# A hybrid pooling and linear-attention block on one core: both head pairs of the state part in step, GpSimd left with weight sums alone, tiles on multiples of 128 bytes

## The chip, the cores and the metric

The kernel runs on one core of a Trainium2 chip. The metric is the time of one execution in microseconds on the device; the median of three runs is given. The core has a matrix engine (TensorE, PE in the profile, with its weight loads as PEld), VectorE (DVE), ScalarE (ACT), GpSimd (POOL), and a queue (SP) that issues all transfers. Each engine works through its own instructions in order and waits on semaphores for the others.

## The reference

```
u = rmsnorm(h, norm_mix);  z = u @ w_in
a, q, k, v, r, lr, ga, gb = split(z)          # 512, 256, 256, 512, 512, 16, 1024, 1024 columns
p   = per group: (trailing mean over 2, 4, 8 or 16 tokens of a) - a;  p = (p @ w_pool_mix) * pool_scale
y_a = p @ w_pool_out
log_a = log_sigmoid(lr @ w_gate_up + b_gate) / 16
# per head (4 heads, 64 key and 128 value columns), over chunks of 64 tokens:
o     = scores_with_decay @ v + (q * exp(b)) @ S;   S = exp(b_end) * S + (k * exp(b_end - b))^T @ v
o   = rmsnorm(o, gla_norm) * silu(r);  y_b = o @ w_gla_out
h   = h + (sigmoid(ga) * y_a + sigmoid(gb) * y_b) @ w_out
h   = h + relu(rmsnorm(h, norm_ffn) @ w_ff1)^2 @ w_ff2
out = rmsnorm(h, norm_final)                  # 1024 tokens, 1024 wide, 16 leading meta tokens dropped
```

## The kernel before

Every large product is made from operands split in two: a high part (`th`, `w1h`, ...), which ACT rounds with a copy, and a low part (`tl`, `w1l`, ...), the difference, which DVE or POOL takes. Three matmuls (L258 to L260: high by high, high by low, low by high) make one product; most are 512 columns wide. A *filler matmul* below is one of these three.

The program runs through these stages. The *opening* (`start`) normalizes eight tiles of 128 tokens, transposes them on PE (L244, identity `ident`), splits them (`th` L200, `tl` L201), and makes the values v, tile by tile (`v_tile`), with the weight halves `vw[0]` and `vw[1]`, which `load_vw` loads through the two `raw` buffers and splits. `lrraw` is sixteen more columns of weights. `warm` makes matmuls of a blank tile. Then come the pooling columns and keys (a ring `W1` of two weight slots is filled by `Ring.top_up`: load, ACT copy L75, subtraction L76 on the engine `W1.eng`). The *pairs of projections* take weights two blocks of 128 columns at a time by a seven-product scheme: `sums_weights` forms sums and differences of weight quarters (`fs`, `s3`, L640 to L646, on POOL), `split` (L598, L599) makes their two parts, three products ahead of use. Between products `inside` runs the decay part of the attention (`gi`, `N`, `F`, L812, L840 to L880), a generator whose pieces are let out by time credits (`STRETCH`). At its end `pooled_part` brings the pooled rows back (`pm_dram`) and splits them into the old `th` and `tl` (L751, L752).

The *state part* (`gla`) runs four units `across(p, half)`: head pair p of 0 and 1, half of the tokens 0 and 1. A unit transposes the keys (L1036), makes the chunk products kv (L1042), runs eight state steps on DVE (L1048), multiplies scores by v (L1055) and queries by states (L1065), squares on ACT (`on`, L1071), reduces (L1073), takes an inverse root (small operations, L209 to L218), scales (L1075), transposes back (L1079), and multiplies by the gate (`sr`, L1080; `yg`, L1082, L1083). At each `yield` it names a time, and `pour` lets out filler matmuls for `PACE` times that long: first the blocks of y_a (`ya_block`: gate exp L950, product with the gate L976, a store to `ma_dram`), then those of y_b for the first half (`yb_block`: L1005, L1006, then `th` and `tl`, L1009 and L1010). Units start one after another, two alive at most:

```
UNITS = [(0, 0), (1, 0), (0, 1), (1, 1)]
...
if waiting and len(live) < 2 and since > 1:
    live.append(waiting.pop(0))
```

The merge, the first feed-forward layer and the second follow; nothing in them is rewritten.

The order on PE is the order of the code. The order on the other engines and on the SP queue is set by a scheduler that works from priorities and readiness, so an edit can move instructions that it does not name. Tiles come from a left-hand stack (from low addresses up) and a right-hand one (from the top down); a tile that is popped gives its place to later ones.

Of the kernel before, what the change touches and what calls it, by code (L numbers as in the profile page):

```python
# [31 lines left out]
PACE, LEVEL, OPENING, STRETCH = 1.6, 1.6, 6.0, 1.9  # L32
# [71 lines left out]
def kernel(  # L104
# [58 lines left out]
    small = left.push("small", [P, 144], F32)  # L163
    small_at = [0]

    def tiny(n):
        a = small_at[0]
        small_at[0] += n
        assert small_at[0] <= 144
        return small[:, a : a + n]  # L170
# [155 lines left out]

    def load_vw(i):
        vw, n = S["vw"][i], 256 + 16 * (i == 0)
        for j in range(2):
            r = raw.load(w_cols(C_V + i * 256 + j * P), D).rearrange("p (k c) -> p k c", k=KT)  # L330
            c = slice(j * P, (j + 1) * P)
            act.activation(vw[:, 0, :, c], r, ACT.Copy)
            eng = pool if i else dve
            eng.tensor_tensor(vw[:, 1, :, c], r, f32(vw[:, 0, :, c]), ALU.subtract)
        if i == 0:
            r = S["lrraw"]
            act.activation(vw[:, 0, :, 256:], r, ACT.Copy)
            pool.tensor_tensor(vw[:, 1, :, 256:], r, f32(vw[:, 0, :, 256:]), ALU.subtract)
# [44 lines left out]
    def start():  # L383
# [3 lines left out]
        S["lrtok"] = left.push("lrtok", [P, 9, 16], F32)  # L387
# [19 lines left out]
        W1.eng = pool  # L407
        for t in range(8):
            if 0 < t < 6:
                load(t + 2)  # L410
            if t == 1:
                nc.sync.dma_start(xm, meta)
            if t == 3:
                W1.top_up()
            u = us[:, t % 3]
            layer_norm(xs[:, t % 4], u)
            transposed(u, t // 4, OFF[t // 4] + (t % 4) * P, ("ms", "sc"))
            if t == 0:
                nc.sync.dma_start(S["lrraw"], w_in[:, C_LR : C_LR + 16].rearrange("(k p) c -> p k c", p=P))
                load_vw(0)  # L420
                load(1)
                load(2)
                load_vw(1)
                warm(10, P)
            if t == 6:
                layer_norm(xm, um)
            if t < 3:
                v_tile(0, t)
            else:
                for i, n in SPREAD[t]:  # L430
                    v_tile(i, n)
# [9 lines left out]
        W1.eng = dve  # L441
# [12 lines left out]
    def pool_open():  # L454
# [11 lines left out]
        pool.tensor_tensor(mw[:, 1], r, f32(mw[:, 0]), ALU.subtract)  # L466
# [51 lines left out]
    def differences():  # L518
# [9 lines left out]
        def parts(p, a, eng=dve):  # L528
            hi, lo = x[p]
            act.activation(hi, a, ACT.Copy)  # L530
            eng.tensor_tensor(lo, a, f32(hi), ALU.subtract)

        dve.tensor_tensor(b11, b12, b11, ALU.subtract)
        pool.tensor_tensor(b12, b22, b12, ALU.subtract)
# [3 lines left out]
        parts("P7", b12, pool)  # L538
# [91 lines left out]
    def sums_weights(order, n_pairs, load, eng):  # L630

        for p, i in order(n_pairs):
# [3 lines left out]
            else:  # L636
                a21, a22 = (w1raw[i, 1][:, k : k + 4] for k in (0, 4))
                s = quad(S["fs"][:, i % 2] if p != "P7" else S["s3"])
                if p == "P5":
                    eng.tensor_tensor(s, a21, a22, ALU.add)  # L640
                elif p == "P6":
                    eng.tensor_tensor(s, s, a11, ALU.subtract)
                elif p == "P7":
                    eng.tensor_tensor(s, a11, a21, ALU.subtract)
                elif p == "P3":
                    eng.tensor_tensor(s, a12, s, ALU.subtract)  # L646
                elif p == "P4":
                    s = a22
# [24 lines left out]
    def pairs_of_projections():  # L673
# [18 lines left out]
        for n, (p, i, (ah, al)) in enumerate(ahead(pair_weights(), 3)):  # L692
# [30 lines left out]
            if n > 8:  # L723
                credit += 12 * 512 / 2400 / STRETCH
                while credit > 0 and chain:
                    w = next(chain, None)
                    if w is None:
                        chain = None
                    else:
                        credit -= w  # L730
# [4 lines left out]
            if total - n == 3:  # L735
                raw.back()
                W1.shift, W1.eng = 1, pool
# [3 lines left out]

    def pooled_part(g):

        S["pm"] = [t[0].rearrange("p k c -> p (k c)")[:, : 4 * SEQ].rearrange("p (g c) -> p g c", g=4) for t in (TH, TL)]
        spare = [t.rearrange("p n b -> p (n b)") for t in (*S["N"], S["F"])]
        for n in range(3) if g == 0 else (3,) if g == 1 else ():
            nc.sync.dma_start(
                spare[n % 3].rearrange("p (h c) -> p h c", h=2), pm_dram[n].rearrange("h p c -> p h c")
            )
        ph, pl = (t[:, g] for t in S["pm"])  # L750
        act.activation(ph, spare[g % 3], ACT.Copy)  # L751
        pool.tensor_tensor(pl, spare[g % 3], f32(ph), ALU.subtract)  # L752
# [141 lines left out]
    UNITS = [(0, 0), (1, 0), (0, 1), (1, 1)]  # L894

    def gla_open():
        W1.eng = pool
# [86 lines left out]
    def yb_block(j, h):  # L984
        def fn(wb):
# [4 lines left out]
            for e in range(2):  # L990
# [19 lines left out]
                pool.tensor_tensor(tl, gl, f32(th), ALU.subtract)  # L1010
# [9 lines left out]
    seen = [tiny(2) for _ in range(2)]  # L1020

    def across(p, half):
# [11 lines left out]
        b = quad(bank("ms"))  # L1034
# [3 lines left out]
        yield 1.6  # L1038
# [10 lines left out]
        yield 4.4  # L1049
# [10 lines left out]
        dve.tensor_copy(seen[p], o[:, :, 3, P - 1])  # L1060
# [15 lines left out]
        yield 6.0  # L1076
# [11 lines left out]
    def gla():  # L1088
# [14 lines left out]
        waiting, live, since = [across(*u) for u in UNITS], [], 9  # L1103
        while waiting or live:
            if waiting and len(live) < 2 and since > 1:
                live.append(waiting.pop(0))
                since = 0
            since += 1
            waits = [(g, next(g, None)) for g in live]
            live = [g for g, w in waits if w is not None]  # L1110
            pour(max([w for _, w in waits if w is not None], default=0) * PACE)
# [6 lines left out]
    def merge_open():  # L1118
        W1.eng = dve
# [298 lines left out]
    tails = [(tiny(1), tiny(1)) for _ in range(4)]  # L1418
# [101 lines left out]
```

## Time and profile before

| | |
|---|---|
| median of 3 runs | 1281.24 us (1277.63 to 1282.63) |
| the profiled execution | 1280.45 us, its span 1278.7 us |
| mean granted TensorE clock | 0.986 |
| busy: PE, DVE, ACT, POOL | 1231.0, 853.4, 634.3, 141.1 us |
| moved | 192 MB, 150 GB/s over the span |

The stages in the profile, by the first instructions of each: opening 0 to 40 us, pooling and keys to 158, pairs of projections to 401 with their last products to 417.5, state part to about 534, merge to 640, then the feed-forward layers. Line numbers are those of the kernel before. A row of the profile names the engine, the line, the tile written and the tiles read. A releaser behind an arrow is what ended the idle time ahead of an instruction.

### The profile page before, as it was taken

To read this page: it belongs to the slowest core of one execution; us is meant where nothing else is said; L and a number is where in the kernel's file an instruction comes from. 1 tells how busy PE (TensorE), PEld (TensorE's weight loads), DVE (VectorE), ACT (ScalarE), POOL (GpSimd) and SP (SyncE) were. 2 spreads that over 40 slices of the span, in tenths; PEclk is the share of its full clock that TensorE was granted. 3 is DMA by queue.
4 is the path that set the end of the run, shared out by engine and by line. 5 is a ranking of instruction groups with operands and counts; after the bars stand their busy time and mean duration, and the time that the engine had idled before them with its cause. 6 is when DMAs were issued, how large, how long until landed. Compare 5 with 4: busy or idle time off the path is not lost.

```text
span 1278.7 us, 18357 instructions
## 1 busy us (share of the span) xinstructions
PE 1231.0 (96%) x6795; PEld 1002.7 (78%) x6795; DVE 853.4 (67%) x1383; ACT 634.3 (50%) x1119; POOL 141.1 (11%) x89
## 2 busy tenths in 40 slices
PE   7999999999998989799999999999999999999997
PEld 6999876777777777588778888888878788888776
DVE  5525459786786356742797767767764777887686
ACT  6623456766666424531665544544554444444544
POOL 2110141222224115410000000000000000000000
PEclk8999999999999999899999999999999999999999
DMA  7312343433336974760234444444469863333532
GB/s 220 111 38 83 93 131 83 122 117 109 101 116 234 320 253 140 246 231 34 83 110 162 149 150 155 149 151 154 156 214 370 268 228 106 98 92 91 166 92 88
DMA packets 153402, 192.23 MB, mean 150 GB/s; under 512 B 12097, under 2 KB 89169, under 8 KB 153313
## 3 DMA queue, kind: packets, MB, share of 16 engines
q1 hardware_dynamic: 153312, 191.06, 46.7%
q8 instruction: 53, 0.87, 0.3%
q14 instruction: 37, 0.30, 0.1%
HBM read 129.14 MB, written 61.88 MB: 149 GB/s over the span
## 4 chain that ended last, share of the span: by engine, by line
PE 79%; DVE 7%; DMA 6%; ACT 4%; issue 3%; POOL 1%; SPq 0%; ACTq 0%; DVEq 0%; POOLq 0%
PE b_o L260 8%; PE b_o L259 8%; PE b_o L258 8%; PE b_mm L259 6%; PE b_mm L260 6%; PE b_mm L258 6%; PE b_y L258 5%; PE b_y L260 5%; PE b_y L259 5%; PE b_z L258 3%; PE b_z L259 3%; PE b_sc L258 3%; PE b_z L260 3%; PE b_sc L259 3%; PE b_sc L260 3%
## 5 line engine op out<-in xcount | busy, mean ns | idle before, releaser
L598 ACT ACTIVATE w1h<-raw 128x512 fp32r<-128x512 f32 x106 | 65.9, 624 | 62.7 <-PE b_y L259 19.5
L599 DVE TENSOR_TENSOR w1l<-raw,w1h 128x512 fp32r<-128x512 f32 x106 | 74.0, 698 | 23.3 <-ACT w1h L598 23.2
L258 PE MATMUL b_sc<-th,w1h 128*128 128x512 f32 x216 | 86.3, 400 | 2.4 <-ACT u2p L705 1.7
L258 PE MATMUL b_z<-th,w1h 128*128 128x512 f32 x216 | 85.9, 398 | 0.0
L259 PE MATMUL b_z<-tl,w1h 128*128 128x512 f32 x216 | 84.9, 393 | 0.4 <-DVE tl L1206 0.4
L259 PE MATMUL b_sc<-tl,w1h 128*128 128x512 f32 x216 | 84.7, 392 | 0.0
L260 PE MATMUL b_z<-th,w1l 128*128 128x512 f32 x216 | 84.6, 392 | 0.0
L260 PE MATMUL b_sc<-th,w1l 128*128 128x512 f32 x216 | 84.6, 391 | 0.0
L258 PE MATMUL b_o<-w1h 128*128 128x512 f32 x192 | 75.8, 395 | 2.9 <-DVE h L1346 1.9
L598 ACT ACTIVATE w1h<-fs 128x512 fp32r<-128x512 f32 x81 | 50.9, 628 | 54.5 <-PE b_y L259 30.8
L259 PE MATMUL b_o<-w1l,w1h 128*128 128x512 f32 x192 | 75.8, 395 | 1.3 <-DVE w1l L599 1.3
L599 DVE TENSOR_TENSOR w1l<-fs,w1h 128x512 fp32r<-128x512 f32 x81 | 60.6, 749 | 23.9 <-ACT w1h L598 23.8
L260 PE MATMUL b_o<-w1h,w1l 128*128 128x512 f32 x192 | 75.9, 395 | 0.1
L258 PE MATMUL b_mm<-th,w1h 128*128 128x512 f32 (+1 forms) x208 | 71.9, 346 | 3.5 <-DVE c L976 2.6
L259 PE MATMUL b_mm<-tl,w1h 128*128 128x512 f32 (+1 forms) x208 | 71.0, 342 | 0.0
L260 PE MATMUL b_mm<-th,w1l 128*128 128x512 f32 (+1 forms) x208 | 71.0, 341 | 0.0
L598 ACT ACTIVATE w1h<-bt 128x512 fp32r<-128x512 f32 x45 | 28.4, 630 | 57.5 <-issue 33.8
L1394 DVE TENSOR_TENSOR bt<-w,w 128x512 f32<-128x512 f32 x80 | 54.8, 685 | 2.4 <-DMA w<-in_w_ff_dram 2.4
L258 PEld LDWEIGHTS b_sc<-th,w1h 128*128 128x128 f32 x216 | 40.6, 188 | 13.4 <-ACT u2p L705 2.1
L258 PE MATMUL b_mm<-wo,th 128*128 128x512 f32 x128 | 50.7, 396 | 0.0
L259 PE MATMUL b_o<-fxl,fxh 128*128 128x512 f32 x128 | 49.8, 389 | 0.6 <-DVE small L217 0.6
L258 PE MATMUL b_o<-fxh 128*128 128x512 f32 x128 | 50.3, 393 | 0.0
(374 smaller groups left out, 3414.2 us busy)
## 6 DMA issues: line engine op xcount, KB each, us to landing
hf_dram<-h SPq DMA_DIRECT2D x112, 256.0 KB, 2.1
raw<-hf_dram SPq DMA_DIRECT2D x112, 256.0 KB, 2.7
w<-in_w_ff_dram SPq DMA_DIRECT2D x64, 256.0 KB, 4.9
raw<-in_w_in_dram SPq DMA_DIRECT2D x22, 512.0 KB, 4.8
raw<-in_w_ff_dram SPq DMA_DIRECT2D x16, 512.0 KB, 4.1
rawx<-in_w_ff_dram SPq DMA_DIRECT2D x16, 512.0 KB, 4.2
rawp<-in_w_in_dram SPq DMA_DIRECT2D x10, 512.0 KB, 4.7
xs<-in_x_dram SPq DMA_DIRECT2D x8, 512.0 KB, 5.5
```

Source lines behind the costliest of these rows:

```text
L258: pe.matmul(ps, ah, bh, start=first and i == 0, stop=False, skip_group_check=more)
L259: pe.matmul(ps, ah, bl, start=False, stop=False, skip_group_check=more)
L260: pe.matmul(ps, al, bh, start=False, stop=last and i == n - 1, skip_group_check=more)
L598: act.activation(hi, a, ACT.Copy)
L599: dve.tensor_tensor(lo, a, f32(hi), ALU.subtract)
L1394: dve.tensor_tensor(bt, w, S["w2"][q[3:]][:, i], ALU.add if q[2] == "+" else ALU.subtract)
```

## The change

It does five things. The units of the state part go in pairs: for each half both `across(0, half)` and `across(1, half)` advance together, and the times named and `PACE` are altered. POOL keeps the sums of weights, each as two instructions of half the width; its subtractions (L76 in the opening and the state part, the second half of `vw` and `lrraw`, L466, L531, L534, L752, L1010) go to DVE. In the opening the weights of `vw[1]` are asked for early and split later, and six more warm matmuls stand after tile 1. `pooled_rows` asks for pooled rows apart from splitting them. `small` shrinks from 144 to 128 columns and `lrtok` grows from 9 to 10 rows, so that left-hand tiles behind them begin on multiples of 128 bytes; two small scratch columns are reused to fit.

```diff
-PACE, LEVEL, OPENING, STRETCH = 1.6, 1.6, 6.0, 1.9
+PACE, LEVEL, OPENING, STRETCH = 1.3, 1.6, 6.0, 1.9
-    small = left.push("small", [P, 144], F32)
+    small = left.push("small", [P, 128], F32)
-        S["lrtok"] = left.push("lrtok", [P, 9, 16], F32)
+        S["lrtok"] = left.push("lrtok", [P, 10, 16], F32)
...
     def load_vw(i):
-            r = raw.load(w_cols(C_V + i * 256 + j * P), D).rearrange("p (k c) -> p k c", k=KT)
+            r = vw_raw[i][j]
-            eng = pool if i else dve
-            eng.tensor_tensor(vw[:, 1, :, c], r, f32(vw[:, 0, :, c]), ALU.subtract)
+            dve.tensor_tensor(vw[:, 1, :, c], r, f32(vw[:, 0, :, c]), ALU.subtract)
...
-        W1.eng = pool
         for t in range(8):
             if t == 0:
-                load_vw(0)
+                ask_vw(0)
                 load(1)
                 load(2)
-                load_vw(1)
                 warm(10, P)
+                load_vw(0)
+                ask_vw(1)
+            if t == 1:
+                warm(6, P)
+            if t == 2:
+                load_vw(1)
...
+        def tt(out, a, b, op):
+            for k in (slice(0, 2), slice(2, 4)) if eng is pool else (slice(0, 4),):
+                eng.tensor_tensor(out[:, k], a[:, k], b[:, k], op)
-                    eng.tensor_tensor(s, a21, a22, ALU.add)
+                    tt(s, a21, a22, ALU.add)
...
     def pooled_part(g):
-        pool.tensor_tensor(pl, spare[g % 3], f32(ph), ALU.subtract)
+        dve.tensor_tensor(pl, spare[g % 3], f32(ph), ALU.subtract)
...
     def gla_open():
-        W1.eng = pool
     def yb_block(j, h):
-                pool.tensor_tensor(tl, gl, f32(th), ALU.subtract)
+                dve.tensor_tensor(tl, gl, f32(th), ALU.subtract)
     def across(p, half):
-        b = quad(bank("ms"))
+        b = quad(bank("ms") if p == 0 else wide2()[:, 0])
-        yield 1.6
+        yield 1.4
-        yield 4.4
+        yield 5.0
-        yield 6.0
+        yield 8.0
     def gla():
-        waiting, live, since = [across(*u) for u in UNITS], [], 9
-        while waiting or live:
-            if waiting and len(live) < 2 and since > 1:
-                live.append(waiting.pop(0))
-                since = 0
-            since += 1
-            waits = [(g, next(g, None)) for g in live]
-            live = [g for g, w in waits if w is not None]
-            pour(max([w for _, w in waits if w is not None], default=0) * PACE)
+        for half in range(2):
+            live = [across(p, half) for p in range(2)]
+            while live:
+                waits = [(g, next(g, None)) for g in live]
+                live = [g for g, w in waits if w is not None]
+                pour(max([w for _, w in waits if w is not None], default=2.0) * PACE)
```

How it moves instructions, at three places. The first is DVE in the opening, from the end of the normalization of tile 1 (`us`) to tile 1's low parts (`tl`); `lrtok` belongs to the first tile of values. Before:

```order
L232 SCALAR_TENSOR_TENSOR us<-xs,small,gB 128x1024
L356 COPY lrtok<-b_mm 128x16
L213 SCALAR_TENSOR_TENSOR small<-small 128x1
L217 TENSOR_SCALAR small<-small 128x1
L218 TENSOR_TENSOR small<-small 128x1
L232 SCALAR_TENSOR_TENSOR us<-xs,small,gB 128x1024
L201 TENSOR_TENSOR tl_135<-b_sc,th_131 128x4x128
L210 TENSOR_SCALAR small<-small 128x1
L201 TENSOR_TENSOR tl_135<-b_ms,th_131 128x4x128
```

The same place on DVE now (`vw_190` is `vw[1]`):

```order
L232 SCALAR_TENSOR_TENSOR us<-xs,small,gB 128x1024
L362 COPY lrtok<-b_mm 128x16
L213 SCALAR_TENSOR_TENSOR small<-small 128x1
L340 TENSOR_TENSOR vw_190<-raw_115,vw_190 128x8x128
L217 TENSOR_SCALAR small<-small 128x1
L210 TENSOR_SCALAR small<-small 128x1
L218 TENSOR_TENSOR small<-small 128x1
L201 TENSOR_TENSOR tl_135<-b_sc,th_131 128x4x128
L201 TENSOR_TENSOR tl_135<-b_ms,th_131 128x4x128
L232 SCALAR_TENSOR_TENSOR us<-xs,small,gB 128x1024
L340 TENSOR_TENSOR vw_190<-raw_119,vw_190 128x8x128
```

One half of `vw[1]` came in ahead of tile 1's low parts, and the normalization of tile 2 went behind them.

The second place is PE at the start of the state part's second unit: `kt_3915` (now `kt_3971`) is the transposed key tile of head pair 1. Before, its kv products followed the first unit's query products:

```order
L1065 MATMUL b_m_4093<-w_3919,gi_3883 64x128 x4
L1065 MATMUL b_m_4093<-S,gi_3883 64x128
L1065 MATMUL b_m_4093<-w_3919,gi_3883 64x128
L1065 MATMUL b_m_4093<-S,gi_3883 64x128
L1065 MATMUL b_m_4093<-w_3919,gi_3883 64x128 x9
L1042 MATMUL b_sc<-v,kt_3915 64x128 x16
```

Now, on PE, they follow the first unit's kv, three products after the keys' transposes:

```order
L1053 MATMUL b_sc<-ident,gi_3943 128x128 x4
L258 MATMUL b_mm<-th_131,w1h 128x512
L259 MATMUL b_mm<-tl_135,w1h 128x512
L260 MATMUL b_mm<-th_131,w1l 128x512
L258 MATMUL b_mm<-th_131,w1h 128x512
L259 MATMUL b_mm<-tl_135,w1h 128x512
L260 MATMUL b_mm<-th_131,w1l 128x512
L258 MATMUL b_mm<-th_131,w1h 128x512
L259 MATMUL b_mm<-tl_135,w1h 128x512
L260 MATMUL b_mm<-th_131,w1l 128x512
L1059 MATMUL b_m_4076<-v,kt_3967 64x128 x16
L1059 MATMUL b_sc<-v,kt_3971 64x128 x16
```

The second unit's kv moved ahead by 33 + 12 filler matmuls and the first unit's last products.

The third place is PE at the end of the last unit: `on_3907` (now `on_3963`) is head pair 1's scaled output, `yg_3875` (now `yg_3931`) the first half's gated outputs and `yg_3871` the second's. Before:

```order
L1065 MATMUL b_sc<-w_3923,gi_3887 64x128 x9
L258 MATMUL b_mm<-yg_3875,w1h 128x512
L259 MATMUL b_mm<-yg_3875,w1h 128x512
L260 MATMUL b_mm<-yg_3875,w1l 128x512
L258 MATMUL b_mm<-yg_3875,w1h 128x512
L259 MATMUL b_mm<-yg_3875,w1h 128x512
L260 MATMUL b_mm<-yg_3875,w1l 128x512
L258 MATMUL b_mm<-yg_3875,w1h 128x512
L259 MATMUL b_mm<-yg_3875,w1h 128x512
L260 MATMUL b_mm<-yg_3875,w1l 128x512
L1079 MATMUL b_sc<-ident,on_3907 128x128 x8
L258 MATMUL b_mm<-yg_3871,w1h 128x512
```

Now, on PE, the rows around both units' last transposes:

```order
L258 MATMUL b_mm<-yg_3931,w1h 128x512
L259 MATMUL b_mm<-yg_3931,w1h 128x512
L260 MATMUL b_mm<-yg_3931,w1l 128x512
L1096 MATMUL b_m_4669<-ident,on_3959 128x128 x8
L1096 MATMUL b_sc<-ident,on_3963 128x128 x8
L258 MATMUL b_mm<-yg_3931,w1h 128x512
L259 MATMUL b_mm<-yg_3931,w1h 128x512
L260 MATMUL b_mm<-yg_3931,w1l 128x512
```

Between the last query products and these transposes stood 9 filler matmuls and now stand 51 (48 in the first half); behind the transposes the second half's outputs were read at once, and now 60 filler matmuls on the first half's outputs come first.

48 lines of the change are left out of this document (27 added, 21 removed).

## The prediction

> **What bounds the kernel now.** I read four views in this order: the head of the page, the busy time by stage (stretches cut where the program changes its loops), the list of who waited for whom on TensorE, and the rows around the longest waits.
>
> ```profile
> span 1278.7 us, 18357 instructions
> ```
>
> ```profile
> core 0: us, PE busy (x) PEld busy (x) DVE busy (x) ACT busy (x) POOL busy (x), PEclk, DMA share, GB/s
> 0.00:40.00 40.00, 33.51 (x188) 27.20 (x189) 20.93 (x45) 27.70 (x58) 12.02 (x12) 0.91 0.74 223
> 40.00:158.00 118.00, 118.00 (x823) 109.04 (x822) 54.01 (x64) 47.45 (x86) 10.49 (x3) 1.00 0.24 70
> 158.00:401.00 243.00, 234.00 (x1788) 180.81 (x1787) 182.40 (x298) 153.40 (x273) 64.81 (x46) 0.99 0.40 121
> 401.00:417.50 16.50, 12.87 (x49) 9.86 (x47) 10.65 (x13) 13.65 (x23) 7.15 (x3) 0.90 0.75 242
> 417.50:534.00 116.50, 102.05 (x753) 80.76 (x754) 66.19 (x111) 46.42 (x70) 34.40 (x18) 0.96 0.73 237
> 534.00:640.00 106.00, 105.62 (x482) 86.14 (x481) 56.19 (x95) 37.81 (x71) 12.20 (x8) 1.00 0.36 127
> 640.00:1278.70 638.70, 624.90 (x2721) 508.88 (x2718) 463.06 (x762) 307.89 (x542) 0.00 (x0) 0.99 0.49 158
> ```
>
> TensorE is the bound nearly everywhere: from 40 to 158 us it never rests, and no work of it is removed. What the change can win is time in which PE stands idle or runs at a lowered clock. Each engine has its busy time and, in brackets, its instructions; the last three columns are the granted clock, the DMA share and the rate. Idle PE is 40.00 - 33.51 = 6.5 us in the opening, 9.0 in the pairs of projections, 3.6 in their last 16 us, and 14.5 us in the state part (417.5 to 534). The clock column adds to that: 0.04 of 116.5 us is 4.7 us more in the state part, 0.1 of 16.5 is 1.7 at the end of the pairs, 0.09 of 40 is 3.6 in the opening.
>
> ```profile
> PE b_sc L1079 <- DVE on L1075: 7.8, 1, 7.8
> PE b_y L258 <- ACT t L556: 2.8, 1, 2.8
> PE b_mm L258 <- DVE c L976: 2.6, 1, 2.6
> PE b_gs L812 <- DVE gi L880: 2.4, 2, 1.7
> PE b_gs L757 <- DVE S L797: 2.2, 2, 1.6
> PE b_mm L260 <- DVE small L210: 2.1, 1, 2.1
> PE b_sc L258 <- ACT u2p L705: 1.7, 1, 1.7
> PE b_mm L259 <- DVE yg L1083: 1.5, 2, 0.8
> ```
>
> Columns: who waited, for what; us in all, times, longest. The first row is the last unit of the state part alone: its transposes (L1079) wait 7.8 us for its normalization, and no filler is left to pour. The third, sixth and second have another thing in common, which the timeline shows:
>
> ```profile
> 17.95 2.36 POOL L334 TENSOR_TENSOR vw<-raw,vw 128x1024 fp32r<-128x1024 f32 x1 [8.84 <-ACT vw L332]
> 18.03 2.30 DVE L213 SCALAR_TENSOR_TENSOR small<-small 128x1 f32<-128x1 f32 x1
> 405.71 2.36 POOL L752 TENSOR_TENSOR tl<-n,th 128x1024 fp32r<-128x1024 f32 x1 [2.15 <-ACT th L751]
> 405.84 2.79 DVE L599 TENSOR_TENSOR w1l<-fs,w1h 128x512 fp32r<-128x512 f32 x1
> 467.35 2.40 POOL L76 TENSOR_TENSOR w1l<-raw,w1h 128x1024 fp32r<-128x1024 f32 x1 [15.15 <-ACT w1h L75]
> 467.74 2.03 DVE L215 TENSOR_TENSOR small<-small 128x8 f32<-128x8 f32 x1 [2.70 <-ACT small L211]
> ```
>
> Each DVE instruction with two SBUF inputs that starts beside a POOL one ends when POOL's ends: one on 128x1 took 2.30 us, one on 128x8 2.03. Each of these three is followed by a PE wait of the list.
>
> **The change, part by part.** Prices:
>
> ```profile
> L76 DVE TENSOR_TENSOR w1l<-raw,w1h 128x1024 fp32r<-128x1024 f32 x6 | 7.6, 1266 | 25.7 <-ACT w1h L75 21.4 <-PE b_sc L258 4.3
> L599 DVE TENSOR_TENSOR w1l<-raw,w1h 128x512 fp32r<-128x512 f32 x106 | 74.0, 698 | 23.3 <-ACT w1h L598 23.2
> L640 POOL TENSOR_TENSOR fs<-raw 128x512 f32<-128x512 f32 x6 | 7.7, 1288 | 51.7 <-DVE w1l L599 45.7 <-issue 6.0
> L338 POOL TENSOR_TENSOR vw<-lrraw,vw 128x128 fp32r<-128x128 f32 x1 | 0.7, 694 | 7.0 <-ACT vw L337 7.0
> ```
>
> *Opening.* POOL's two halves of vw1, its lr columns and two W1 parts go to DVE: 4 x 1.27 + 0.7 = 5.8 us more on an engine that is busy 20.9 of 40. The first is placed behind the small operations of tile 2 and before tile 1's tl, but the 2.30 us block goes, so tile 1's tl ends about 1.5 us earlier; ACT also takes th before the second half of vw1. Six 128-column warm matmuls fill PE's wait there.
>
> ```profile
> 20.00:24.00 4.00, 1.83 (x8) 1.61 (x9) 3.47 (x8) 2.89 (x7) 2.95 (x2) 0.63 0.79 240
> 24.00:28.00 4.00, 4.00 (x20) 4.00 (x20) 1.89 (x4) 1.32 (x3) 0.27 (x1) 0.51 0.60 190
> ```
>
> In those 8 us the clock column loses 0.49 x 4 = 2.0 us while PE works throughout, and 0.37 x 4 = 1.5 while it works less than half of the time, some 0.4 of it on work. Without an idle PE these 2.4 go, and 1.5 of the idle time: 3.9, less 0.4 for warm matmuls that outlast the wait. I take -3.5; ends -1.5 (clock falls all the same) and -4.5. From 40 us PE is full, so it is kept.
>
> *Pairs.* 44 POOL sums of 128x512 become 88 of 128x256. One of 256 columns lies between 694 and 1288 ns, so a pair costs 1.4 to 2.6 us against 1.29; POOL is busy 64.8 of 243 us, and the sums are made three products (8 us) ahead, which hides it, except for the first sum (L705's wait of 1.7): +0.2. A blocked DVE operation now waits out half an instruction. Of the waits here (2.4 + 2.2 and less) only the 1.7 on gi follows a block; I take -1.5 net; ends +1 and -5 (all these waits, and part of the clock).
>
> *End of the pairs.* The four pooled tl (L752) go to DVE, 4 x 1.27 = 5.1 us, against blocks like the 2.79 (2.1 too long). In the new order w1l<-fs stands before the last tl, u2p, which frees the bank, behind it: PE's 2.8 us wait shrinks to about 2.8 - 2.1 + 0.7 = 1.4. The clock around it:
>
> ```profile
> 408.00:412.00 4.00, 2.63 (x8) 2.15 (x9) 3.21 (x5) 2.83 (x5) 1.13 (x2) 0.77 0.64 227
> 412.00:416.00 4.00, 4.00 (x16) 3.21 (x15) 1.29 (x2) 3.78 (x6) 1.32 (x1) 0.80 0.97 282
> 480.00:484.00 4.00, 3.20 (x8) 2.32 (x9) 3.84 (x9) 1.57 (x2) 2.48 (x1) 0.73 0.60 169
> 484.00:488.00 4.00, 4.00 (x29) 3.11 (x29) 2.04 (x4) 1.69 (x2) 1.28 (x1) 0.84 0.92 279
> ```
>
> (0.23 + 0.20) x 4 = 1.7 us, lost behind a wait of 2.8; 1.7 again behind the yg waits at 480. I count 1.1 of the first: -2.5, ends 0 and -5. The Trainium skill (TensorE: Matmul & The Clock Gate, Part 1) lets the clock halve only after an idle window of about 3.4 us; by that rule stalls of 2.8 and 1.5 us would cost no clock, and only the 7.8 us stall's share would be won, which makes the sum 3 to 4 us smaller. These rows show the fall behind waits shorter than that, so I keep it.
>
> *State part.* Full removal is worth 14.5 us of idle and about 3.4 of clock (4.7 less what fell inside the stall), 17.9. In step, each half has both units' normalization behind 48 and 51 filler matmuls, and 60 filler matmuls follow the last transposes, where before there were 9 and none (the order shown above). At the spacing of
>
> ```profile
> 794.77 0.39 PE L258 MATMUL b_y<-wo,w1h 128*128 128x512 f32 x1
> 797.27 0.39 PE L260 MATMUL b_y<-wo,w1l 128*128 128x512 f32 x1
> 800.21 0.40 PE L258 MATMUL b_y<-t4h,w1h 128*128 128x512 f32 x1
> 802.78 0.40 PE L260 MATMUL b_y<-t4h,w1l 128*128 128x512 f32 x1
> ```
>
> (12 matmuls each; 2.50 / 11 = 0.227 and 2.57 / 11 = 0.234 us) 48 are 10.9 us. Two normalizations need about 10, an estimate: two reductions and two scalings of 128x1024 at 1.27, two ACT squares of about 1, two rows of small operations of some 1.5. What comes new:
>
> ```profile
> L1042 PE MATMUL b_m<-v,kt x32: 269/269/320, 427.7 to 428.5; 64*64 64x128 f32 x32
> 424.54 2.34 SPq L917 DMA_DIRECT2D v<-v_dram  x3
> DMA to landing us min/median/max: 6.0/6.8/8.2
> ```
>
> The second unit's kv comes right behind the first's, at about 428.5 on the old clock, and its v is the first of three issued from 424.54: landed at 430.5 to 431.3. +2. From the second half's last state product on, DVE has 8 gate blocks of three operations (24 x 0.69 = 16.6), 5 W1 parts (6.3) and 8 operations of 128x1024 for the tails (10): 33 us, against 111 matmuls and 16 transposes on PE, 27. Three mm banks and what stood ready absorb half: +3. DMA moved 0.73 of its time over 116 us and moves the same in 100, with x's reload issued earlier: late gates and a clock step, +3. So -17.9 + 8 = -10; ends -3 and -17.
>
> *Alignment.* By the built programs the left-hand tiles start 64 bytes past a multiple of 128 before and on one after; right-hand tiles (t4) stay 96 past. The rows above have both operands on the left (0.227) and one on each side (0.234); pairs that agree go on agreeing, and mixed ones stay mixed. I take 0; ends: the 7 ns between the two rows on the 3203 matmuls from 534 us, 22 us either way, improbable.
> The Trainium skill (DMA: Bandwidth & Descriptors, How a descriptor splits into AXI transactions) lets a transfer that starts off a 256-byte boundary pay an extra transaction; by it left tiles that land on such a boundary would be cheaper, about a ninth at 2 KB, and the sum unchanged while PE waits for no transfer. No row here has an aligned tile to test it.
>
> Sum: -3.5 - 1.5 - 2.5 - 10 = -17.5. The profiled execution took 1280.45 us, 0.8 below the median of 1281.24; against the median that is 1263.5.
>
> **Rivals.** (a) *Late gates and DVE in the state part eat most of it*: DVE busy would rise from 66 of 116 us by 8 W1 parts and 16 tl, 21 us, and PE waits for banks; state -3, the rest as above less half of the clock: 1280 - 9 = 1272. For it speaks the 0.73 DMA share; against it that DVE loses the blocks. (b) *Slower*: DVE, strictly in order, becomes the bound from 480 to 534. Its 33 us over 27 would have to be 33 + 18 to undo the rest; that needs every DVE operation there to wait 0.5 us for an ACT or PE partner: 1284. (c) *All of it*: opening 4.5, pairs 5, end 5, state 17: 1249. (d) *The alignment acts*: every left-left matmul moves by a few ns; half of the 22 us on top of the sum, 1252, or against it, 1275. (e) *The step does not do what it says*: both units in step only wait for each other, the last wait stays at 7.8 for a pair: 1263.5 + 7.8 = 1271; the 48 and 51 matmuls ahead of it speak against it.
>
> **How the numbers follow.** Forecast 0.57 (1257 to 1270), a 0.17, b 0.04, c 0.11, d 0.06, e 0.05. To leave out no more than 2 in 10, the range runs from 1251, which leaves c's lower half outside, to 1275. 0.5% is 6.4 us, about what a measurement of this kernel can tell from no change: faster than 1274.8 are the forecast, c, most of a and d: 0.88; within 0.08; slower 0.04.
>
> **What would show it.** Right: no DVE row of 128x1 or 128x8 over 0.7 us; granted clock 1.0 between 20 and 28 us; no wait over 3 us for `on`; idle PE in the state part 5 to 9 us; matmul spacing 0.227 and 0.234 as before. Wrong: PE waits on mm banks or W1 parts totalling over 8 us behind the second half, ACT idle for gates with PE idle beside it, or a spacing that moved.

## The result and the profile after

The changed kernel takes 1260.74 us (median of 4 runs, 1259.17 to 1261.23) against 1280.55 us before on the same chip: a ratio of 0.9845, 95% interval 0.9823 to 0.9867, so 19.8 us less. (With a fourth run the median of the kernel before is 1280.55; the forecast was worked out from the 1281.24 of three.) The forecast of 1263.5 us was 2.8 us too high, and the range of 1251 to 1275 held it. The profiled execution took 1261.11 us.

The head of the page of the changed kernel:

```profile
span 1259.2 us, 18413 instructions
PE 1223.6 (97%) x6807; PEld 998.9 (79%) x6807; DVE 865.8 (69%) x1421; ACT 634.6 (50%) x1119; POOL 74.1 (6%) x95
```

The span is 19.5 us shorter. PE's busy time was 1231.0 us before (the sum of the seven stages shown ahead of the prediction), so 7.4 us of the 19.5 are less time with matmuls in flight (the mean granted clock rose from 0.986 to 0.994), and 12.1 are idle time that went. The busy time by stage, with the stretches cut at the same matmuls as in the table ahead of the prediction (from the second row on the counts on PE agree within one):

```profile
core 0: us, PE busy (x) PEld busy (x) DVE busy (x) ACT busy (x) POOL busy (x), PEclk, DMA share, GB/s
0.00:37.70 37.70, 31.87 (x200) 25.90 (x201) 22.48 (x50) 27.22 (x57) 1.37 (x7) 1.00 0.78 232
37.70:155.70 118.00, 118.00 (x823) 109.11 (x822) 59.13 (x67) 47.95 (x88) 0.00 (x0) 1.00 0.24 71
155.70:396.30 240.60, 232.38 (x1788) 179.86 (x1787) 179.59 (x301) 155.18 (x275) 72.70 (x88) 0.99 0.42 124
396.30:409.30 13.00, 11.59 (x49) 8.66 (x47) 10.01 (x14) 10.69 (x19) 0.00 (x0) 1.00 0.75 239
409.30:512.30 103.00, 97.90 (x754) 80.38 (x755) 68.24 (x123) 42.70 (x65) 0.00 (x0) 0.98 0.79 258
512.30:620.20 107.90, 106.17 (x481) 85.76 (x480) 63.51 (x109) 42.98 (x78) 0.00 (x0) 1.00 0.39 138
620.20:1259.20 639.00, 625.67 (x2721) 509.27 (x2719) 462.80 (x762) 307.85 (x542) 0.00 (x0) 0.99 0.48 158
```

In the state part (409.3 to 512.3) PE now idles 103.00 - 97.90 = 5.1 us, where it was 14.5, and the clock is 0.98 instead of 0.96. At the end of the pairs it idles 1.4 us instead of 3.6, at full clock. The pairs (155.7 to 396.3) still lose 8.2 us, where it was 9.0, and the merge behind the state part now idles 1.7 us, where it was 0.4. PE's longest waits:

```profile
PE b_m L1059 <- ACT kt L1054: 2.6, 2, 2.1
PE b_gs L832 <- DVE gi L900: 1.9, 2, 1.1
PE b_sc L258 <- ACT u2p L718: 1.8, 1, 1.8
PE b_o L258 <- DVE h L1359: 1.7, 1, 1.7
PE b_gs L777 <- DVE S L817: 1.7, 2, 1.1
PE b_sc L1059 <- DMA v<-v_dram: 1.6, 1, 1.6
```

The wait of 7.8 us for `on` is gone. So are the first gate product's 2.6 us for c and the pairs' last 2.8 us for t. New are kt, copied on ACT behind a gate's exponential (two waits, 2.1 us the longest), and v.

Three groups of instructions that both kernels have show how the lead grows. Each row gives first and last start; before first (L258, L1042, L1177), then the changed kernel:

```profile
L258 PE MATMUL b_y<-t0h,w1h x44: 389/393/628, 166.4 to 403.0; 128*128 128x512 f32 x44
L1042 PE MATMUL b_m<-v,kt x64: 269/269/320, 427.7 to 474.9; 64*64 64x128 f32 x64
L1177 DVE TENSOR_TENSOR acc<-b_mm,acc x16: 682/691/692, 548.8 to 643.3; 128x512 f32<-128x512 f32 x16
```

```profile
L258 PE MATMUL b_y<-t0h,w1h x44: 389/389/501, 164.4 to 398.3; 128*128 128x512 f32 x44
L1059 PE MATMUL b_m<-v,kt x64: 269/269/414, 419.9 to 459.9; 64*64 64x128 f32 x64
L1190 DVE TENSOR_TENSOR acc<-b_mm,acc x16: 679/691/692, 527.2 to 623.5; 128x512 f32<-128x512 f32 x16
```

At the start of the pairs the lead is 2.0 us, near their end 4.7, at the first state product 7.8, at the first sum of the merge 21.6, at its last 19.8, at the end 19.5. By stage: opening 2.0, pairs 2.7, end of pairs 3.1, state part and merge 12.0 (the state part 13.8, of which the merge gives back 1.8), and 0.3 given back. These leads are one execution against one.

### The profile page after: what moved, and what is told of

Its sections match the earlier page's. It is cut to its first block, busy times and chain, and to the rows that moved or that the text cites. A ratio compares the mean times of both kernels' runs of the same rounds, so it can differ in the third digit from the quotient of the medians.

```text
span 1259.2 us, 18413 instructions
## 1 busy us (share of the span) xinstructions
PE 1223.6 (97%) x6807; PEld 998.9 (79%) x6807; DVE 865.8 (69%) x1421; ACT 634.6 (50%) x1119; POOL 74.1 (6%) x95
## 4 chain that ended last, share of the span: by engine, by line
PE 72%; DMA 10%; DVE 9%; ACT 5%; issue 3%; SPq 1%; POOL 0%; DVEq 0%; ACTq 0%; POOLq 0%
PE b_o L259 7%; PE b_o L260 7%; PE b_o L258 7%; PE b_mm L258 6%; PE b_mm L260 6%; PE b_mm L259 5%; PE b_y L258 5%; PE b_y L260 5%; PE b_y L259 5%; PE b_z L258 3%; PE b_z L259 3%; PE b_sc L258 3%; PE b_z L260 3%; PE b_sc L259 3%; PE b_sc L260 3%
## 5 line engine op out<-in xcount | busy, mean ns | idle before, releaser
L607 ACT ACTIVATE w1h<-raw 128x512 fp32r<-128x512 f32 x106 | 66.0, 624 | 57.8 <-PE b_sc L259 19.5
L258 PE MATMUL b_sc<-th,w1h 128*128 128x512 f32 x216 | 86.2, 399 | 2.4 <-ACT u2p L718 1.8
L258 PE MATMUL b_z<-th,w1h 128*128 128x512 f32 x216 | 85.6, 396 | 0.7 <-DVE c L726 0.7
L258 PE MATMUL b_o<-w1h 128*128 128x512 f32 x192 | 75.5, 393 | 2.7 <-DVE h L1359 1.7
L258 PE MATMUL b_mm<-th,w1h 128*128 128x512 f32 (+1 forms) x208 | 72.3, 348 | 0.9 <-DVE c L734 0.9
L608 DVE TENSOR_TENSOR w1l<-fs,w1h 128x512 fp32r<-128x512 f32 x81 | 56.9, 703 | 23.0 <-ACT w1h L607 22.9
L258 PEld LDWEIGHTS b_sc<-th,w1h 128*128 128x128 f32 x216 | 40.5, 188 | 13.7 <-ACT u2p L718 2.2
L258 PE MATMUL b_mm<-wo,th 128*128 128x512 f32 x128 | 50.6, 395 | 0.0
L260 PE MATMUL b_o<-fxh,fxl 128*128 128x512 f32 x128 | 50.4, 393 | 0.0
```

Source lines behind the costliest of these rows:

```text
L258: pe.matmul(ps, ah, bh, start=first and i == 0, stop=False, skip_group_check=more)
L260: pe.matmul(ps, al, bh, start=False, stop=last and i == n - 1, skip_group_check=more)
L608: dve.tensor_tensor(lo, a, f32(hi), ALU.subtract)
```

## The experiments

All times are set against the kernel before on the same chip. The changed kernel itself was run twice, and its two ratios (0.9845 and 0.9827) show how far a comparison across chips can be trusted. No run undoes the moves of L466, L531 and L534 to DVE.

| kernel | median us | ratio to before | 95% interval |
|---|---|---|---|
| changed | 1260.74 | 0.9845 | 0.9823 to 0.9867 |
| changed, again | 1257.47 | 0.9827 | 0.9803 to 0.9851 |
| changed, units staggered as before | 1269.55 | 0.9925 | 0.9899 to 0.9951 |
| before, units in step | 1276.70 | 0.9972 | 0.9953 to 0.9992 |
| changed, GpSimd back in the state part | 1274.81 | 0.9958 | 0.9935 to 0.9981 |
| changed, GpSimd writing to no reader there | 1269.78 | 0.9898 | 0.9868 to 0.9928 |
| changed, opening as before | 1259.12 | 0.9845 | 0.9814 to 0.9877 |
| changed, old offsets | 1257.37 | 0.9802 | 0.9778 to 0.9826 |
| changed, whole weight sums | 1257.99 | 0.9828 | 0.9799 to 0.9856 |
| changed, weight sums on DVE | 1251.00 | 0.9744 | 0.9709 to 0.9778 |
| changed, v first and kt on DVE | 1258.07 | 0.9808 | 0.9779 to 0.9837 |
| the last two together | 1251.88 | 0.9777 | 0.9752 to 0.9802 |
| the same, old offsets | 1249.89 | 0.9774 | 0.9750 to 0.9797 |

**The step undone.**

```
-PACE, LEVEL, OPENING, STRETCH = 1.3, 1.6, 6.0, 1.9
+PACE, LEVEL, OPENING, STRETCH = 1.6, 1.6, 6.0, 1.9
...
-        b = quad(bank("ms") if p == 0 else wide2()[:, 0])
+        b = quad(bank("ms"))
...
-        for half in range(2):
-            live = [across(p, half) for p in range(2)]
...
+        waiting, live, since = [across(*u) for u in UNITS], [], 9
...
```

The yields of 1.4, 5.0 and 8.0 go back to 1.6, 4.4 and 6.0.

> The changed kernel with the four units of the state part staggered as before (its order, pace, yields and bank); GpSimd's part and the alignment stay as changed. Theory 1, the step wins the state part's time because fillers cover the normalizations: the wait of the last transposes for the normalized rows comes back with 7 to 8 us, and with the two units' smaller waits the time is 1268 to 1272 us; idle PE in the state part rises from 6.7 to 14 us or more. Theory 2, the normalization was long only because GpSimd held DVE's operations: the wait comes back with 4 us or less and the time is 1262 to 1265 us.

It measured 1269.55 us, 9 to 12 us more than the changed kernel: theory 1. PE's longest waits in the state part:

```profile
PE b_sc L1097 <- DVE on L1093: 6.0, 1, 6.0
PE b_mm L258 <- ACT yg L1100: 2.6, 2, 1.4
```

The wait for `on` is back, with no GpSimd instruction anywhere near it. It is 6.0 us rather than 7.8, so freeing DVE took 1.8 us off that wait and no more; the fillers that the step puts ahead of it do the rest.

**The step alone.** The kernel before with the same edits the other way round.

> The kernel before with both head pairs in step and nothing else of the change. Theory 1: the wait of 7.8 us goes, GpSimd's blocks stay; the state part gives some 9 of its 13 us and the rest nothing, 1270 to 1273 us. Theory 2: with GpSimd's subtractions of 2.4 us beside it the paired normalization outlasts its 48 to 51 filler matmuls, waits of 3 us or more stand before the transposes of both halves, 1276 to 1281 us.

It measured 1276.70 us, only 4.0 us under the kernel before. The time is in theory 2's range, but not at theory 2's place: no wait for `on` appears among its longest. They are

```profile
PE b_y L258 <- DVE u2p L709: 2.7, 1, 2.7
PE b_mm L258 <- DVE c L1005: 2.7, 1, 2.7
PE b_m L1042 <- ACT kt L1037: 2.5, 1, 2.5
PE b_mm L258 <- ACT w1h L75: 2.4, 1, 2.4
```

The step took its wait away, and new ones stand at the gate products behind the second half (c, w1h). Its PE waits between 507 and 533 us add up to 8.6 us (2.72, 0.82, 1.58, 2.37, 1.12); in the changed kernel those behind the second half up to the merge are 2.1 (0.78, 0.80, 0.53). The step alone gives 4 us (0.9972), the rest of the change alone 10 (0.9925), both together 20 to 22: some 7 us belong to neither alone, and the 6.5 us between these two sums of waits are most of them.

**GpSimd back in the state part.** Opening, step, half-width sums and offsets as changed.

```
-                W1.shift = 1
+                W1.shift, W1.eng = 1, pool
...
-        dve.tensor_tensor(pl, spare[g % 3], f32(ph), ALU.subtract)
+        pool.tensor_tensor(pl, spare[g % 3], f32(ph), ALU.subtract)
...
     def gla_open():
+        W1.eng = pool
...
-                dve.tensor_tensor(tl, gl, f32(th), ALU.subtract)
+                pool.tensor_tensor(tl, gl, f32(th), ALU.subtract)
...
     def merge_open():
+        W1.eng = dve
```

The gated rows (`tl`) are those of both halves, so eight of GpSimd's subtractions lie in the merge, as in the kernel before.

> The changed kernel with GpSimd's subtractions back from the end of the pairs to the end of the state part (pooled tl, gate tl, low parts of W1); opening, step and half-width sums stay as changed. Theory 1, GpSimd's instructions hold DVE's operations: DVE rows of 128x1 or 128x8 over 2 us come back, PE waits behind them at the end of the pairs and in the state part, 3 to 4 us and 2 to 4 us, so 1265 to 1268.5 us. Rival: filler and banks cover the blocks now that the units run in step, and DVE has 16 us less to do: 1259 to 1263 us.

It measured 1274.81 us, 14 to 17 us more than the changed kernel. That is above theory 1's range: it had the direction and about half of the size. Its rival falls. The timeline behind the second half, POOL's rows and DVE's beside them:

```profile
501.86 2.64 POOL L76 TENSOR_TENSOR w1l<-raw,w1h 128x1024 fp32r<-128x1024 f32 x1 [5.03 <-ACT w1h L75]
502.20 0.68 DVE L1024 TENSOR_TENSOR c<-b_mm,c 128x512 f32<-128x512 f32 x1
502.92 2.13 DVE L1025 TENSOR_TENSOR c<-c 128x512 f32<-128x512 f32 x1
...
509.18 2.39 POOL L76 TENSOR_TENSOR w1l<-raw,w1h 128x1024 fp32r<-128x1024 f32 x1
509.48 2.64 DVE L1025 TENSOR_TENSOR o<-o 128x512 f32<-128x512 f32 x1
...
518.63 1.06 ACT L1161 ACTIVATE wo<-raw 128x1024 fp32r<-128x1024 f32 x1 [4.14 <-POOL tl L1029]
519.73 1.23 DVE L1162 TENSOR_TENSOR wo<-raw,wo 128x1024 fp32r<-128x1024 f32 x1 [5.89 <-ACT wo L1161]
```

Two costs are to be seen. DVE's additions with both inputs in SBUF take 2.13 and 2.64 us beside POOL's 2.4, while the multiplication whose first input is a PSUM bank takes its 0.68 in the middle of one. The two long additions end 0.55 us behind the POOL instruction: they wait it out and then run. And POOL's own queue runs late: ACT stands 4.14 us for a `tl` of POOL, and DVE, its next operation being of that ACT result, 5.89 us. In the changed kernel the same stretch of DVE is packed without a gap:

```profile
497.88 0.68 DVE L1023 TENSOR_TENSOR c<-b_mm,c 128x512 f32<-128x512 f32 x1
...
507.95 0.68 DVE L1024 TENSOR_TENSOR c<-c 128x512 f32<-128x512 f32 x1
```

Sixteen operations start between these two times inclusive, fourteen that take 0.60 us from start to start and two W1 parts that take 1.13, and none waits. This is the burst that the step makes: the gate blocks and W1 parts of the fillers follow one another behind the second half, DVE has little slack there, so most of what GpSimd adds to a DVE operation is passed on. That fits the 7 us that belong to neither part alone, though no run took the burst alone away.

**GpSimd writing to no reader.** To part the two costs: DVE makes every low part, and GpSimd subtracts the high parts of W1 and of the gated rows from themselves into an unused tile.

```
             self.eng.tensor_tensor(lo, raw, hi.bitcast(F32), ALU.subtract)
+            if self.beside is not None:
+                self.nc.gpsimd.tensor_tensor(self.beside, hi.bitcast(F32), hi.bitcast(F32), ALU.subtract)
...
+                if not h:
+                    pool.tensor_tensor(ML[1][:, 0], f32(th), f32(th), ALU.subtract)
```

> The changed kernel, DVE making every low part as changed, and beside each low part of W1 (128x1024) and of the gated rows of the first half (128x512) in the state part GpSimd subtracts the same high part from itself into a tile that nobody reads: the result waits for nothing of GpSimd. Theory 1, what GpSimd costs in the state part is that it holds DVE's operations beside it: DVE rows of 2 us and more come back, and with them 4 to 9 us of time, 1265 to 1270 us. Rival, what cost 14 us in the run with GpSimd in the state part was that the low parts themselves came late from a slower engine with a queue of its own: 1260 to 1262.5 us here.

It measured 1269.78 us: theory 1. Groups from 413 to 532 us (mean of one in ns behind the comma), this kernel's first and the changed kernel's behind:

```profile
L79 POOL TENSOR_TENSOR tl<-w1h 128x1024 fp32r<-128x1024 f32 x8 | 18.5, 2312 | 77.6 <-ACT w1h L76 77.3
...
L77 DVE TENSOR_TENSOR w1l<-raw,w1h 128x1024 fp32r<-128x1024 f32 x9 | 13.7, 1526 | 2.7 <-ACT w1h L76 2.7
...
L1032 DVE TENSOR_TENSOR tl<-o,th 128x512 fp32r<-128x512 f32 x3 | 4.6, 1527 | 0.0
```

```profile
L76 DVE TENSOR_TENSOR w1l<-raw,w1h 128x1024 fp32r<-128x1024 f32 x10 | 12.2, 1220 | 9.1 <-ACT w1h L75 9.1
...
L1028 DVE TENSOR_TENSOR tl<-o,th 128x512 fp32r<-128x512 f32 x4 | 2.7, 682 | 0.0
```

DVE's operations rise from 682 to 1527 ns in the group of gated rows shown (the two other groups to 1187 and 1248) and from 1220 to 1526, with nothing depending on GpSimd's results. By the ratios that costs 7 to 9 us, against 14 to 17 when DVE's work itself was on GpSimd. What makes up the rest is not shown: GpSimd has 16 instructions here, 8 W1 parts and 8 gated rows, and had 30 there (10, 16 and 4 pooled rows), so some of it can be more holding. That its own queue runs late shows only in ACT's wait of 4.14 us above.

The Trainium skill (SBUF — State Buffer, Who interferes with whom) says that a DVE instruction with two SBUF inputs contends with a GpSimd instruction that reads SBUF, that what they share is locked by one at a time, the order of issue deciding who blocks, and that a DVE instruction with at most one SBUF input, outside the two-port modes, does not contend. The rows agree: 2.13 and 2.64 us with two SBUF inputs, 0.68 us with one.

**The opening undone.**

```
+        W1.eng = pool
...
                 ask_vw(0)
+                load_vw(0)
                 load(1)
                 load(2)
+                ask_vw(1)
+                load_vw(1)
                 warm(10, P)
-                load_vw(0)
-                ask_vw(1)
...
-            if t == 1:
-                warm(6, P)
-            if t == 2:
-                load_vw(1)
...
```

POOL also subtracts for `vw[1]` and the lr columns again.

> The changed kernel with the opening of before: GpSimd takes the second v weight's two halves, the lr columns and the low parts of W1 there, no warm matmuls behind tile 1, and the loads in the old order. Theory 1, the opening's gain is kept to the end because PE is full from 40 us on: the 2.1 us by which PE is ahead at the opening's end come back whole, 1262 to 1264 us, and the granted clock falls between 20 and 28 us. Rival: a later wait takes the 2.1 us in, 1260 to 1261.5 us.

It measured 1259.12 us, between the two runs of the changed kernel and below the ranges of both theories: theory 1 is not borne out. Its opening is the old one, clock and all:

```profile
0.00:36.50 36.50, 30.16 (x166) 24.25 (x167) 18.21 (x37) 24.68 (x49) 11.49 (x11) 0.91 0.76 238
```

So the lead of 2 us at the opening's end is there in the profile after, and at the end of the program it can't be told from nothing. In this profile PE is 1.6 us behind the changed kernel's first profile at the start of the pairs (`b_y<-t0h,w1h` at 166.0 against 164.4) and 1.8 near their end, but only 0.4 at the first state product (420.3 against 419.9), and 2.0 ahead at the merge's first sum (525.2 against 527.2), which the second profile of the changed kernel reaches at 521.8. The medians put its worth between -1.6 and +1.7 us, and the intervals leave room for some 4 us; whether a part of it lasts stays open.

**The offsets, twice.**

```
-    small = left.push("small", [P, 128], F32)
+    small = left.push("small", [P, 144], F32)
-        S["lrtok"] = left.push("lrtok", [P, 10, 16], F32)
+        S["lrtok"] = left.push("lrtok", [P, 9, 16], F32)
```

> The changed kernel with its two small tiles at their old sizes (144 and 9 x 16 columns), so that every tile on the left begins 64 bytes past a multiple of 128 again; nothing else differs. Theory 1, the alignment does nothing: the time of the changed kernel, 1259 to 1262.5 us, matmul spacing 0.228 us where both operands are at one offset. Rival, aligned tiles are what brings part of the 20 us: 1266 us or more.

1257.37 us, a ratio of 0.9802, under the changed kernel's on another chip. That left open whether aligned tiles cost something, so the pair was run on one chip, on the version without GpSimd's sums:

> The kernel run beside it (sums on DVE, v first, k's copy on DVE) with the two small tiles at their old sizes, so that the left-hand tiles begin 64 bytes past a multiple of 128: the alignment by itself, on one chip beside its partner. Theory 1: no effect, within 2 us of its partner either way. Rival, suggested by the earlier run with old offsets (1257.4 against 1260.7 us of the changed kernel on another chip): the aligned tiles cost something, and this one is 3 us or more faster than its partner.

0.9774 against 0.9777: the alignment has no effect that can be seen. The single times (1248.8 to 1253.6 us and 1247.2 to 1254.6) leave room for some 2 us.

**Whole weight sums.**

```
-            for k in (slice(0, 2), slice(2, 4)) if eng is pool else (slice(0, 4),):
+            for k in (slice(0, 4),):
```

> The changed kernel with GpSimd's weight sums whole again (44 of 128x512, 1.29 us each in the profile before, instead of 88 halves), all else as changed. Theory 1, what the sums cost is the time that GpSimd runs beside DVE, 57 us instead of 73: DVE is held for less, 1 to 3 us faster than the changed kernel. Rival, the length of one instruction decides, since a held operation waits out the instruction beside it: waits for gi and S grow back, 1 to 3 us slower than the changed kernel.

0.9828 against 0.9827 for the changed kernel on the same chip: neither effect is seen. The single times (1256.8 to 1259.0 us and 1255.1 to 1259.5) leave room for some 2 us, so the smaller end of either theory is not ruled out.

**No weight sums on GpSimd.**

```
-        S["pw"] = sums_weights(pairs_order, len(PAIRS), load_pair, pool)
+        S["pw"] = sums_weights(pairs_order, len(PAIRS), load_pair, dve)
```

> The changed kernel with the weight sums of the pairs on DVE too, full width; GpSimd then does nothing from 36 us on. DVE has 44 x 0.69 = 30 us more in the 243 us of the pairs, 212 busy. Theory 1: the half-width blocks cost as little as DVE's new work, PE waits on sums or w1l nowhere by more than 1 us: 1259 to 1262.5 us. Rival: DVE falls behind in the pairs, waits for S, gi and w1l grow: 1264 to 1269 us.

1251.00 us: both theories were wrong, and on the slow side. DVE takes on 44 operations and the kernel gets faster. The stretch from 154 to 397 us, the changed kernel's row first and this one's behind, and the wait for gi in this kernel:

```profile
154.00:397.00 243.00, 234.78 (x1799) 181.80 (x1798) 181.82 (x302) 156.48 (x278) 72.70 (x88) 0.99 0.41 123
154.00:397.00 243.00, 239.77 (x1822) 186.07 (x1821) 201.30 (x353) 163.12 (x287) 0.00 (x0) 0.99 0.42 129
```

```profile
PE b_gs L832 <- DVE gi L900: 0.6, 1, 0.6
```

PE idles 3.2 us in these 243, not 8.2, and gets to the end of the pairs 5.1 us earlier (the last `b_y<-t0h,w1h` at 393.2 against 398.3). DVE is 19.5 us busier, not 30, and has 51 instructions more in the stretch: the rest it gets back because nothing is held. One operation of the same line in the same burst, in the changed kernel beside two halves on POOL, and here:

```profile
206.07 1.88 POOL L643 TENSOR_TENSOR s<-rawp,rawp 128x256 f32<-128x256 f32 x2 [5.15 <-DVE w1l L608]
...
207.28 1.22 DVE L871 TENSOR_TENSOR n<-n,ends 128x512 f32<-128x512 f32 x1
```

```profile
205.90 0.67 DVE L871 TENSOR_TENSOR n<-n,ends 128x512 f32<-128x512 f32 x1
```

In the changed kernel DVE is 75% busy over the pairs, but in this burst it runs back to back, and PE's scan products behind it (L832) stand 1.28 us at 211.7 (put down to ACT's t) and 1.14 at 216.6 (to DVE's gi). Here the first wait is gone and the second is 0.6.

**v first, k's copy on DVE; then all together.**

```
-        act.activation(kt, b, ACT.Copy)
+        dve.tensor_copy(kt, b)
...
+        load_v(0)
         ask()
+        load_v(1)
```

`load_v` loads the v rows of one half; the first now stands between the first fetches and the first gate loads (`ask`).

> The changed kernel with two more edits, in search of a better one: the v rows of the first half are loaded ahead of the gate loads (PE waits 1.6 us for them), and the copy of the transposed k goes from ACT, where it stands behind a gate's exponential that waits for its load (PE waits 2.1 us, and the granted clock falls behind it), to DVE. Theory 1: both waits go, with 1.7 us of clock, 1255.5 to 1258 us. Rival: the loads of the state part set its end, and the waits move to the gates: 1260 to 1262 us.

1258.07 us, between the ranges of the two theories and not to be told from the changed kernel. The wait for v left the list and kt's fell to 0.6 us, but waits of 1.8 us for a gate's c and 1.4 us for a copy of two columns of the score products (`small`) stood there instead.

> The run with the weight sums on DVE and the one with v first and k's copy on DVE put together, in search of the best. Theory 1: the edits work on different waits and add: 1247.5 to 1250 us. Rival: the sums' gain of some 8 us already moved the state part's waits, and nothing is added to 1251: 1250 to 1252.5 us.

1251.88 us, so the rival: nothing is added to the run with the sums on DVE. On the same chip as the changed kernel it and its twin with old offsets are 5.6 and 7.6 us faster (0.9777 and 0.9774 against 0.9827). The best version found is therefore the changed kernel with nothing left on GpSimd, about 1250 us.

**The changed kernel again.**

> The changed kernel itself once more, so that the three runs beside it are compared on one chip: 1258 to 1262 us, and a ratio to before of 0.982 to 0.987. If it is below 1258.5 us here, the faster times of the runs with old offsets and with v first are the chip and not the edit.

1257.47 us, below the 1258.5 of its expectation: the faster times of the runs with old offsets and with v first, on another chip, need no effect of their edits. For the offsets the pair above shows it on one chip; v first was not run beside the changed kernel.

## Why the prediction was right, and where not

*The sum.* -17.5 was forecast, -19.5 came, in the terms' own order: opening -3.5 against -2.0; pairs -1.5 against -2.7; end of the pairs -2.5 against -3.1 up to the first state product; state part -10 against -12.0 with the merge; rest 0 against +0.3. Every term is inside its ends. That the sum is so close is partly luck, as the next points show, and the shares hold for this execution: in the second profile of the same kernel PE leads by 1.3 us at the start of the pairs (behind a fall of the clock that is shown below), 5.5 near their end, 9.8 at the first state product, 25.3 behind the merge and 25.4 at the end.

*Opening.* The prediction let the clock recover and the six warm matmuls fill the wait, and that happened:

```profile
20.00:24.00 4.00, 3.47 (x25) 3.03 (x25) 3.51 (x8) 3.97 (x10) 0.00 (x0) 1.00 0.52 130
24.00:28.00 4.00, 2.61 (x20) 2.16 (x19) 3.64 (x8) 2.94 (x8) 0.00 (x0) 1.00 0.98 329
```

Idle time of 1.4 us stays in the second window, so -3.5 was over-sized by 1.5, in its idle time first of all: over the whole opening that fell from 6.5 to 5.8 us, 0.7 where 1.5 was counted. "From 40 us PE is full, so it is kept" holds to the pairs; that it is kept to the end was not shown by the run without it.

*Pairs.* The term landed, the reasoning did not. The step that failed is "which hides it": GpSimd's sums are ready in time, but they are not hidden, because they lengthen DVE's operations in a burst that PE waits for. Taking them away (with v first and kt on DVE, which add nothing) is worth 5.6 to 7.6 us on one chip, where the whole term was -1.5 with -5 as the best case. Splitting them in two, the part of the change that the term was about, shows no effect.

*End of the pairs.* PE's wait of 2.8 us for t is gone, and the clock stays at 1.00 there, where 1.1 of 1.7 us had been counted. The reading that it rests on, "ends when POOL's ends", holds for the two small operations shown there; the row of 2.79 us ends 0.56 us behind POOL's.

*State part.* The prediction counted 17.9 us of idle time and clock, and asked 8 back. The run with the step undone bears out the filler argument: 48, 51 and 60 matmuls cover the normalizations. What was missing is that the step and GpSimd's leaving are not two terms. The prediction put GpSimd's share at blocks of 2 us that end in single waits; the step alone was worth 4 us and GpSimd's leaving the state part, with the step in place, 14 to 17. The rivals named DVE's extra work as the danger (a, b). DVE did become packed behind the second half, as rival b said, but unheld it keeps up, which is the reason that was given against rival a: it took on 10 W1 parts and 16 low parts, 10 x 1.22 + 16 x 0.68 = 23 us, and its busy time in state part and merge rose only from 122.4 to 131.8 us, so some 14 us of it had been time in which it was held. The +3 for DVE's packed end came as the 2.1 us of waits named above, part of them in the merge.

*New waits.* v was counted at +2 and measured 1.6. kt was not foreseen: its copy stands on ACT behind the exponential of a gate that has not landed. Behind that wait the clock falls:

```profile
456.00:460.00 4.00, 1.87 (x35) 1.45 (x37) 1.25 (x2) 2.51 (x4) 0.00 (x0) 0.89 0.86 224
460.00:464.00 4.00, 4.00 (x48) 3.31 (x41) 3.79 (x10) 0.04 (x1) 0.00 (x0) 0.69 0.99 362
```

(0.11 + 0.31) x 4 = 1.7 us, behind a wait of 2.1. In the second run of the same kernel this wait is below 1 us and the clock is 1.00 there, but it loses the same 1.7 us at another place:

```profile
156.00:160.00 4.00, 2.19 (x6) 1.66 (x6) 1.22 (x1) 1.11 (x2) 3.37 (x6) 0.76 0.94 229
160.00:164.00 4.00, 4.00 (x16) 3.23 (x15) 2.27 (x3) 2.27 (x4) 2.54 (x4) 0.81 0.14 35
```

The length of the wait alone does not say whether it falls. In the first profile it also fell here, behind 0.6 us without work (240 to 244):

```profile
244.00:248.00 4.00, 4.00 (x12) 3.13 (x12) 0.70 (x2) 2.57 (x6) 0.63 (x1) 0.57 0.17 66
```

In the second profile the same 0.6 us left it at 1.00. The Trainium skill (TensorE: Matmul & The Clock Gate, Part 1) asks for an idle window of about 3.4 us. As in the kernel before, the clock fell here behind waits of about 2 us and less, so the measurement decides: keeping the clock's share in the sum was right.

*Alignment.* 0 was taken with 22 us either way as ends; two kernels on one chip differ by 0.0003 of the time. The spacing stayed, and so did the difference between operands on one side and on two (changed kernel, twelve rows from the first to the second, ten from the third to the fourth):

```profile
774.84 0.39 PE L258 MATMUL b_y<-wo,w1h 128*128 128x512 f32 x1
...
777.33 0.39 PE L260 MATMUL b_y<-wo,w1l 128*128 128x512 f32 x1
...
780.28 0.40 PE L258 MATMUL b_y<-t4h,w1h 128*128 128x512 f32 x1
...
782.39 0.39 PE L258 MATMUL b_y<-t4h,w1h 128*128 128x512 f32 x1
```

2.49 / 11 = 0.226 and 2.11 / 9 = 0.234 us.

*What would show it.* No 128x1 or 128x8 operation over 0.7 us, clock 1.0 from 20 to 28 us, no wait over 3 us for `on`, 5 to 9 us idle in the state part (5.1), spacing as before: all came.

## What to carry to other kernels

An engine that works beside DVE is not free because its own results are in time: look at what each of its instructions does to DVE's durations, row by row, and above all in bursts where DVE runs back to back and TensorE waits, since the average share of busy time hides them. Here every step of moving GpSimd's element-wise work to DVE, down to the last, paid or was neutral, though DVE got more to do. And price two edits that pack and unpack the same stretch together: apart they gave 4 and 10 us, together 20.

## What the runs showed of the hardware

- A DVE operation with both inputs in SBUF took 2.1 to 2.6 us beside a GpSimd subtraction of 2.4 to 2.6, and 0.68 without. With one input in PSUM it took 0.68 beside the same instruction.
- The hold runs both ways: in the changed kernel the groups of half-width sums on GpSimd take 0.74 to 0.97 us in the mean (0.94 in the pair shown above); a pair with no DVE operation beside it, at 156.2 us, took 1.41, so 0.71 each.
- Two profiled executions of the same program spanned 1259.2 and 1253.3 us. Where the clock falls changes from one to the next, 1.7 us each time, and a wait for kt of 2.1 us in one is 0.7 in the other. A single profile can't settle a term of 2 us in this kernel.
- Matmuls of 512 columns start 0.226 us apart where both operands lie on the left and 0.234 us where one lies on the other side, whatever the multiple of 64 bytes at which the left side begins.
